# Strassen's seven block products for the down projections of two MLPs and a gated network, in fp32 made of three fp32r products

## The chip, the cores and the metric

One core of one Trainium2 chip runs the whole program. The time is device microseconds of one execution; a kernel's time is the median of its runs.

## The reference

A first block of depth 2 (an even mixer of latent attention and sliding-window attention, an odd mixer of forgetting attention, each followed by an MLP and a gate), then a second block (gated linear attention and a convolution, followed by a gated network). All is float32 over 512 rows of 1024 columns. What the change touches are the three products that take hidden activations back to 1024 columns:

```
def _sq_relu_mlp(x, w_up, w_down):
    return jnp.square(jax.nn.relu(x @ w_up)) @ w_down
...
        x = _layer_norm(DN_ALPHA * x + _sq_relu_mlp(x, w_up[i], w_down[i]), ln2_g[i], ln2_b[i])
...
        h2 = rmsnorm(x, norm2_g[l])
        ffn = (jax.nn.silu(h2 @ w_ffn_gate[l]) * (h2 @ w_ffn_up[l])) @ w_ffn_down[l]
        x = x + ffn
```

`w_up` is 1024 x 4096, `w_down` 4096 x 1024 (twice); the gated network has 2816 hidden columns.

## The kernel before, in words

A float32 matrix is kept as two fp32r ones: hi, a cast made by ScalarE, and lo, the remainder, a subtraction made by VectorE (`split`, L312; the cast is L269, the subtraction L280). A float32 product is three TensorE matmuls, hi x hi, hi x lo and lo x hi (`mm3`, L243; every one is L241), added up in one of eight PSUM banks.

A small planner writes the order of the instructions at build time. Each piece of work is a Python generator (`Core.spawn`) that yields what it waits for; `Core.run` (L362) keeps a clock per engine from assumed costs and takes the next step by when its conditions are met, with a look-ahead of 1400 ns, VectorE and ScalarE work ahead of TensorE work. The engines then run what was written, each in its own order, and wait on semaphores. Memory comes from arenas of columns: `ar_t` and later `ax_r` for fp32r (L495: NR = 118 x 256 and NX = 24 x 256 columns), `af_t` for float32.

`Weights` (L409) brings weights in the order of a plan: `loads` (L425) issues a 512 KB DMA on SyncE into a raw float32 tile while fewer than `rawcap` (2) are held, `preps` (L440) splits a raw tile into a unit (hi and lo, 1024 columns each, 2048 columns in all) while fewer than `cap` units are in use, `get` and `done` hand it out and take it back. Four units are fixed; more come from the arena if there is room. In the MLPs the cap is 8.

An MLP (`mlp`, L1279) goes in four quarters of 1024 hidden columns, called parts here; the gated network (`ffn`, L1996) in three, of 8, 8 and 6 column tiles. So there are 4 + 4 + 3 = 11 parts. In a part, first eight tiles of 128 hidden columns are made for all 512 rows: eight triples of matmuls by `fm` (L580), then `up_ev` (L1292): relu on ScalarE out of PSUM, square on VectorE, split into H (the tile's hi and lo, 512 columns each). Then the products: for each half of the output columns (h) and each block of 128 rows (t), `tm` (L593) makes eight triples of 128x512 matmuls with H as the stationary operand and eight weight tiles moving, 24 matmuls a block, 192 a part. `resid` (L626) adds the block to the residual in `xt` on VectorE (L294). Behind the last part `ln_finish` (L614) normalizes, and a gate layer follows.

Of the kernel before, what the change touches and what calls it, by code (L numbers as in the profile page):

```python
# [17 lines left out]
D = 1024  # L18
# [125 lines left out]
class Core:  # L144
# [91 lines left out]
    def mm(self, out, lhsT, rhs, start, stop):  # L236
# [4 lines left out]
        self.nc.tensor.matmul(out, lhsT, rhs, start=start, stop=stop)  # L241

    def mm3(self, out, sh, sl, mh, ml, start, stop):  # L243
        self.mm(out, sh, mh, start, False)
        self.mm(out, sh, ml, False, False)
        self.mm(out, sl, mh, False, stop)
# [162 lines left out]
class Weights:  # L409


    def __init__(self, core, cap):
        self.c, self.cap = core, cap
        self.plan, self.units, self.inuse = [], {}, 0
        self.raws = {}
        self.rawcap, self.closed = 2, False
        self.fixed = [core.ar.take(2048, 0) for _ in range(4)]
        self.home = list(self.fixed)
        self.rawfix = [core.af.take(1024, 0) for _ in range(2)]
        self.rawhome = list(self.rawfix)  # L420

    def add(self, key, src, d0, d1):
        self.plan.append((key, src, d0, d1))

# [14 lines left out]

    def preps(self):  # L440
        c = self.c
        i = 0
        while True:
            yield ("x", [lambda: len(self.plan) > i or self.closed])
            if i == len(self.plan):
                return
            key, src, d0, d1 = self.plan[i]
            i += 1
            n = d0 * d1
            yield ("x", [lambda: key in self.raws and self.inuse < self.cap])  # L450
            self.inuse += 1
            raw = self.raws[key]
# [12 lines left out]
            if raw in self.rawfix:  # L465
                self.rawhome.append(raw)
            else:
                raw.free()
            del self.raws[key]
# [17 lines left out]
def model_kernel(ctx: ExitStack, tc: tile.TileContext, a: dict, dbg=None):  # L487
# [7 lines left out]
    NR, NF, NS, NX = 118 * 256, 60 * 256, 4 * 256, 24 * 256  # L495
# [782 lines left out]

    def mlp(i, pT):  # L1279
        pT["b"] = yield from c.allocs(R, 1024, 2)  # L1280
        H = (yield from c.allocs(R, 1024, 8))
        hv = [z.v(2) for z in H]

        def hcols(n, t):
            return [(z[:, 0, tb(t)], z[:, 1, tb(t)]) for z in hv[:n]]

        he = {}
        g = yield from bcast(a["ln2_g"][i], D)
        b_ = yield from bcast(a["ln2_b"][i], D)
        st = [small(12) for _ in range(NB)]  # L1290

        def up_ev(b, f, e, dn):  # L1292
# [6 lines left out]
            c.split(hv[f][:, 0], hv[f][:, 1], r.ap)  # L1299
# [5 lines left out]
        ev = None  # L1305
        e0 = [[None] * 4, [None] * 4]
        for q in range(4):
            es = [Event() for _ in range(8)]
            f0 = 0
            if q == 0:  # L1310
                f0 = 4
                yield from first([("up", i, 0, f) for f in range(f0)],
                                 lambda n, b: c.spawn(up_ev(b, n, es[n], dn_done), 0))
            for f in range(f0, 8):
                w = yield from W.get(("up", i, q, f))
                b = yield from fm(w, 0, 128, A["x"], 8, A["ev"])
                W.done(("up", i, q, f))
                c.spawn(up_ev(b, f, es[f], dn_done), 0)
            if q == 3:
                ev = refresh_A()  # L1320
                c.spawn(pT_load(i, pT), 400)
            dn_done = Event()
            for h in range(2):
                keys = [("dn", i, q, h, u) for u in range(4)]
                for t in range(NB):
                    b = yield from tm(hcols(8, t), keys, 512, es, t == 3)
                    last = q == 3
                    post = (lambda t=t: ln_finish(t, st[t], g.ap, b_.ap, ev[t])) if last and h else None
                    e = Event()
                    pre = [x for x in (e0[h][t], e0[0][t] if h else None) if x is not None]  # L1330
                    c.spawn(resid(b, t, h, ALPHA if q == 0 else 1.0, st[t] if last else None,
                                  lambda pre=pre: all(x.on for x in pre), post, e), 0)
                    e0[h][t] = e
            dn_done.set()
        for z in H:
            z.free()
# [8 lines left out]
    def pT_load(i, st):  # L1345
        pb = st["b"]
# [649 lines left out]
    def ffn():  # L1996
        H = (yield from c.allocs(R, 1024, 8))
        hv = [z.v(2) for z in H]

        def hcols(n, t):  # L2000
            return [(z[:, 0, tb(t)], z[:, 1, tb(t)]) for z in hv[:n]]

        nf = yield from bcast(a["norm_f_g_2"], D)
        e0 = [[None] * 4, [None] * 4]
# [11 lines left out]
        def up_ev(b, st, f, e, dn):  # L2016
# [3 lines left out]
            c.give(b)  # L2020
            yield ("x", [r.ap])
            c.split(hv[f][:, 0], hv[f][:, 1], r.ap)
            r.free()
            e.set()

        for q in range(3):
            nk = 8 if q < 2 else 6
            es = [Event() for _ in range(nk)]
            f0 = 0
            if q == 0:  # L2030
                f0 = 2
                sts = [{"e": Event()} for _ in range(f0)]

                def evac(n, b):
                    f = n // 2
                    c.spawn(up_ev(b, sts[f], f, es[f], dn_done) if n % 2 else silu_ev(b, sts[f]), 0)

                yield from first([(nm, f) for f in range(f0) for nm in ("fg", "fu")], evac)
            for f in range(f0, nk):
                st = {"e": Event()}  # L2040
                for nm in ("fg", "fu"):
                    w = yield from W.get((nm, q * 8 + f))
                    b = yield from fm(w, 0, 128, A["x"], 8, A["ev"])
                    W.done((nm, q * 8 + f))
                    c.spawn(silu_ev(b, st) if nm == "fg" else up_ev(b, st, f, es[f], dn_done), 0)
            dn_done = Event()
            for h in range(2):
                keys = [("fd", q, h, u) for u in range(nk // 2)]
                for t in range(NB):
                    b = yield from tm(hcols(nk, t), keys, 512, es, t == 3)  # L2050
                    post = (lambda t=t: rms_out(t, nf.ap)) if q == 2 and not h else None
                    e = done2[t] if q == 2 and h else Event()
                    pre = [y for y in (e0[h][t], e0[0][t] if h else None) if y is not None]
                    c.spawn(resid(b, t, h, 1.0, None, lambda pre=pre: all(y.on for y in pre), post, e), 0)
                    e0[h][t] = e
            dn_done.set()

    def plan_ffn():
        for q in range(3):
            nk = 8 if q < 2 else 6  # L2060
            for f in range(nk):
                W.add(("fg", q * 8 + f), a["w_ffn_gate_2"][q * 8 + f], 8, 128)
                W.add(("fu", q * 8 + f), a["w_ffn_up_2"][q * 8 + f], 8, 128)
            for h in range(2):
# [4 lines left out]
    def plan_mlp(i):  # L2069
        for q in range(4):  # L2070
            for f in range(8):
                W.add(("up", i, q, f), a["w_up"][i, q * 8 + f], 8, 128)
            for h in range(2):
# [150 lines left out]
```

## Time and profile before

| | |
|---|---|
| median of three runs | 1889.79 us (1889.46 to 1891.51) |
| the profiled execution, its own time | 1889.55 us |
| its span | 1887.8 us |
| TensorE matmul busy | 1868.2 us, 99% of the span |
| VectorE, ScalarE busy | 1019.2 us (54%), 714.5 us (38%) |
| mean granted TensorE clock | 0.996 of full speed |

Durations below are those of the profiled execution. PE is TensorE, PEld its weight loads, DVE VectorE, ACT ScalarE. Matmuls are pipelined, so a record of twelve is 0.16 us longer than the distance to the next twelve; the distance is what a matmul costs. An engine's busy share is an average over stages with different limits, so stages are read by themselves.

### The profile page before, as it was taken

The page shows a single profiled execution, that of the slowest core. Times are in us where ns is not written, and L with a number is a line of the kernel's source. Part 1 is how long each engine was busy: PE and PEld are TensorE (multiplying, and loading weights), DVE is VectorE, ACT ScalarE, POOL GpSimd, SP SyncE. Part 2 cuts the span into 40 slices and gives each one's busy share as a digit, 9 for nine tenths or more (in the row PEclk, how much of TensorE's full clock was granted, in tenths as well). Part 3 has the DMA queues.
Part 4 walks back from the last instruction along what each step waited for, and adds up shares of the span by engine and source line. Part 5 has one row for each costly group of instructions (what it writes and reads, how often), then busy time and mean ns, then how long its engine had stood idle before and what let it go on. Part 6 is the DMA issues. An engine that isn't in the chain of part 4 may idle for free.

```text
span 1887.8 us, 23458 instructions
## 1 busy us (share of the span) xinstructions
PE 1868.2 (99%) x9354; PEld 1563.2 (83%) x9354; DVE 1019.2 (54%) x1677; ACT 714.5 (38%) x1242; POOL 62.3 (3%) x123
## 2 busy tenths in 40 slices
PE   9999999999999999989999999999999999999998
PEld 7876788888888888878988888888889898888887
DVE  4666763433447577777734343476675563333333
ACT  4567242323333365553414132333543243132232
POOL 1000100000001000000000000011010000000000
PEclk9999999999999999999999999999999999999999
DMA  5201343232322222222323232332222343133221
GB/s 175 79 32 55 112 136 100 90 111 67 123 90 87 72 79 89 90 90 89 128 85 123 79 111 90 100 112 71 90 90 79 101 134 101 67 123 101 89 90 45
DMA packets 53741, 178.16 MB, mean 94 GB/s; under 512 B 6456, under 2 KB 9072, under 8 KB 53632
## 3 DMA queue, kind: packets, MB, share of 16 engines
q1 hardware_dynamic: 53632, 176.67, 28.7%
q8 instruction: 73, 1.20, 0.3%
q14 instruction: 36, 0.29, 0.1%
HBM read 174.50 MB, written 2.14 MB: 94 GB/s over the span
## 4 chain that ended last, share of the span: by engine, by line
PE 94%; DVE 3%; POOL 1%; ACT 1%; DMA 1%; issue 0%; SPq 0%; POOLq 0%; ACTq 0%; DVEq 0%
PE ps_t L241 91%; PE ps_t L250 3%; DVE ar_t L280 1%; DVE af_t L294 1%; DVE sm_t L631 1%; POOL sm_t L555 0%; POOL sm_t L554 0%; ACT ar_t L269 0%; DMA af_t<-in_ev_w_kv 0%; DMA af_t<-ed 0%; SPq L310 0%; ACT af_t L265 0%; DVE ar_t L289 0%; DVE af_t L280 0%; DVE sm_t L616 0%
## 5 line engine op out<-in xcount | busy, mean ns | idle before, releaser
L241 PE MATMUL ps_t<-ar_t 128*128 128x512 f32 (+5 forms) x6801 | 1430.5, 367 | 9.7 <-DVE ar_t L280 4.1
L241 PEld LDWEIGHTS ps_t<-ar_t 128*128 128x128 f32 x6801 | 1174.0, 189 | 212.0 <-DVE ar_t L280 6.1
L280 DVE TENSOR_TENSOR ar_t<-af_t,ar_t 128x1024 fp32r<-128x1024 f32 (+7 forms) x370 | 402.9, 1097 | 393.8 <-ACT ar_t L269 390.3
L269 ACT CAST ar_t<-af_t 128x1024 fp32r<-128x1024 f32 (+7 forms) x370 | 348.5, 950 | 671.1 <-PE ps_t L241 458.3
L241 PE MATMUL ps_t<-ar_t,ax_r 128*128 128x512 f32 (+1 forms) x1392 | 335.0, 388 | 0.0
L241 PEld LDWEIGHTS ps_t<-ar_t,ax_r 128*128 128x128 f32 x1392 | 259.6, 188 | 53.1
L294 DVE SCALAR_TENSOR_TENSOR af_t<-af_t,ps_t 128x512 f32<-128x512 f32 (+2 forms) x152 | 98.9, 653 | 212.2 <-PE ps_t L241 206.4
L269 ACT CAST ar_t<-ps_t 64x512 fp32r<-64x512 f32 (+4 forms) x169 | 84.9, 521 | 169.7 <-PE ps_t L250 100.9
L280 DVE TENSOR_TENSOR ar_t<-ps_t,ar_t 64x512 fp32r<-64x512 f32 (+4 forms) x169 | 99.6, 607 | 74.8 <-ACT ar_t L269 73.6
L280 DVE TENSOR_TENSOR af_t<-ps_t,af_t 128x512 f32<-128x512 f32 (+1 forms) x82 | 56.1, 686 | 45.8 <-PE ps_t L241 28.3
L280 DVE TENSOR_TENSOR af_t<-af_t 128x512 f32<-128x512 f32 (+2 forms) x105 | 68.0, 648 | 8.1 <-ACT af_t L265 6.6
L269 ACT CAST ax_r<-af_t 128x512 fp32r<-128x512 f32 (+2 forms) x62 | 38.3, 618 | 86.1 <-DVE af_t L280 84.9
L250 PE MATMUL ps_t<-ident,af_t 128*128 128x128 f32 (+1 forms) x496 | 70.2, 273 | 0.4 <-DVE af_t L294 0.3
L294 DVE SCALAR_TENSOR_TENSOR af_t<-af_t,sm_t 128x512 f32<-128x512 f32 x80 | 56.6, 749 | 24.8 <-POOL sm_t L555 17.8
L265 ACT ACTIVATE af_t<-ps_t 128x512 f32<-128x512 f32 (+2 forms) x110 | 58.2, 530 | 26.4 <-PE ps_t L241 26.2
L250 PEld LDWEIGHTS ps_t<-ident,af_t 128*128 128x128 f32 (+1 forms) x496 | 58.0, 139 | 9.7 <-DVE af_t L294 2.5
L265 ACT ACTIVATE af_t<-af_t 128x512 f32<-128x512 f32 (+4 forms) x48 | 31.6, 667 | 89.7 <-DVE af_t L280 50.0
L554 POOL TENSOR_SCALAR sm_t<-sm_t 128x1 f32<-128x1 f32 (+1 forms) x40 | 17.8, 444 | 1403.9 <-DVE sm_t L616 1107.5
L280 DVE TENSOR_TENSOR ax_r<-af_t,ax_r 128x512 fp32r<-128x512 f32 (+2 forms) x62 | 42.6, 687 | 37.2 <-ACT ax_r L269 37.1
L269 ACT COPY af_t<-ps_t 128x512 f32<-128x512 f32 (+4 forms) x75 | 39.9, 562 | 43.8 <-PE ps_t L241 29.7
L265 ACT ACTIVATE af_t<-af_t,sm_t 128x128 f32<-128x128 f32 (+3 forms) x76 | 42.2, 557 | 23.6 <-DVE sm_t L731 19.2
L241 PE MATMUL ps_t<-af_t,ax_f 128*64 128x256 f32 (+6 forms) x136 | 39.4, 418 | 0.6 <-DMA af_t<-ed 0.6
(97 smaller groups left out, 579.0 us busy)
## 6 DMA issues: line engine op xcount, KB each, us to landing
af_t<-in_w_up SPq DMA_DIRECT2D x64, 512.0 KB, 3.4
af_t<-in_w_down SPq DMA_DIRECT2D x64, 512.0 KB, 3.3
af_t<-in_w_ffn_gate SPq DMA_DIRECT2D x22, 512.0 KB, 3.4
af_t<-in_w_ffn_up SPq DMA_DIRECT2D x22, 512.0 KB, 3.5
af_t<-in_w_ffn_down SPq DMA_DIRECT2D x22, 512.0 KB, 3.4
af_t<-in_ple_w_gate SPq DMA_DIRECT2D x16, 512.0 KB, 3.3
af_t<-in_ev_w_out SPq DMA_DIRECT2D x8, 512.0 KB, 4.1
af_t<-in_od_w_q SPq DMA_DIRECT2D x8, 512.0 KB, 3.5
```

The lines of the kernel that those rows point to most:

```text
L241: self.nc.tensor.matmul(out, lhsT, rhs, start=start, stop=stop)
L250: self.nc.tensor.transpose(out, src, ident)
L265: self.nc.scalar.activation(out, src, func, **kw)
L269: self.nc.scalar.copy(out, src)
L280: self.nc.vector.tensor_tensor(out, a, b, op=op)
L294: self.nc.vector.scalar_tensor_tensor(out, a, s, b, op0=op0, op1=op1)
L554: c.pool(165, [src], [v]).tensor_scalar(out=v, in0=src, scalar1=scale, scalar2=eps, op0=ALU.mult, op1=ALU.add)
L631: c.vec(602, [xt[t][:, hs(h)]], [s6]).bn_stats(s6, xt[t][:, hs(h)])
```

## The change

Eight of the eleven parts (all but the last of each MLP and of the gated network) make their products by Strassen's scheme in Winograd's form. The part's 512 x 1024 hidden block is seen as 2 x 2 blocks of 256 rows and 512 columns, its weight as 2 x 2 blocks of 512 x 512. Seven block products of sums of blocks take the place of eight; each is 2 row halves x 4 column tiles x 3 matmuls.

On the hidden side the column tiles come in pairs (`PAIRS`, 0 with 2, 1 with 3, 4 with 6, 5 with 7); relu and square are both on ScalarE, and `Hidden.sums` makes, for each pair, the splits of the three plain blocks (256 and 512 columns), four sums of 256 columns and their split (1024). On the weight side `Weights.add_seven` keeps eight raw tiles, makes eight subtractions in place on VectorE and splits fourteen units. `seven` makes the products in the order 1, 2, 5, 3, 6, 7, 4 (called products 1 to 7), some going on in a bank that an earlier one has filled, and adds to the residual sixteen times. The `rawcap` is 10 in these parts, the norm's gain and bias are loaded ahead of the last part's products instead of at the MLP's start, `af_t` grows from 60 to 75 x 256 columns, and the tiles for the gate's small projection are taken in the last part.

```
+    def add_seven(self, nm, src):
+        for r, c in ((0, 0), (1, 0), (0, 1), (1, 1)):
+            for g in range(2):
+                self.plan.append((nm + (r, c, g), src(r, c, g), 2, 512))
...
+        b11, b12, b21, b22 = (0, 0), (0, 1), (1, 0), (1, 1)
+        for m, z in ((1, b11), (2, b21)):
+            for g in range(2):
+                split(m, z, g)
+        for g in sub(b11, b12, b11):
+            split(5, b11, g)
+        for g in range(2):
+            split(3, b22, g)
+        for g in sub(b11, b22, b11):
+            split(6, b11, g)
+        for g in sub(b12, b22, b12, (b22,)):
+            split(7, b12, g, True)
+        for g in sub(b21, b21, b11, (b11,)):
+            split(4, b21, g, True)
...
     def preps(self):
...
+            if kind == "sub":
+                d, x, y, free = op
...
+                c.tt(ds, xs, ys, ALU.subtract)
...
+        def sums(self, j, ra, rb, e, dn):
+            hi, lo = self.own[0][j], self.own[1][j]
+            sb = yield from c.alloc(F, 1024)
+            yield ("x", [ra.ap, rb.ap, dn])
+            x, y, z = ra.ap, rb.ap, sb.v(4)
+            c.split(hi[:, 0:256], lo[:, 0:256], x[:, 0:256])
+            c.split(hi[:, 256:768], lo[:, 256:768], y)
+            c.tt(z[:, 0], x[:, 256:512], y[:, 256:512], ALU.add)
+            c.tt(z[:, 2], x[:, 0:256], x[:, 256:512], ALU.subtract)
+            c.tt(z[:, 1], z[:, 0], x[:, 0:256], ALU.subtract)
+            c.tt(z[:, 3], y[:, 0:256], z[:, 1], ALU.subtract)
...
+            c.split(self.sum[0][j], self.sum[1][j], sb.ap)
...
+    def hidden():
+        big = yield from c.allocs(R, 1024, 8)
+        return Hidden(big, (yield from c.allocs(R, 768, 8)))
...
+        def add(self, t, h, src):
+            s, pre, e = self.next(t, h)
+            yield ("x", [pre, src])
+            c.stt(xt[t][:, hs(h)], xt[t][:, hs(h)], s, src, ALU.mult, ALU.add)
...
+        for m, bs in ((1, x), (2, p)):
+            for t in range(2):
+                bs[t] = yield from part(m, t, None, range(3), True)
...
+        for m, bs in ((1, x), (2, p)):
+            for t in range(2):
+                yield from part(m, t, bs[t], [3], False)
+                c.spawn(give(None if m == 1 else bs[t], [acc.add(t, 0, c.pb(bs[t]))], xe[t] if m == 1 else None), 0)
+            done(m)
+        for t in range(2):
+            z[t] = yield from part(5, t, None, range(4), True)
+            c.spawn(give(None, [acc.add(t + 2, 1, c.pb(z[t]))], ze[t]), 0)
+        done(5)
+        for t in range(2):
+            yield from part(3, t, z[t], range(4), False, [ze[t]])
+            c.spawn(give(z[t], [acc.add(t, 1, c.pb(z[t]))]), 0)
+        done(3)
...
+        for t in range(2):
+            yield from part(6, t, x[t], range(4), False, [xe[t]])
+            c.spawn(keep(t), 0)
+        done(6)
+        for t in range(2):
+            yield from part(7, t, x[t], range(4), False, [ue[t]])
+            c.spawn(give(x[t], [acc.add(t + 2, 0, c.pb(x[t])), acc.add(t + 2, 1, c.pb(x[t]))]), 0)
+        done(7)
+        for t in range(2):
+            b = yield from part(4, t, None, range(4), True)
+            c.spawn(give(b, [acc.add(t + 2, 0, c.pb(b))]), 0)
...
     def mlp(i, pT):
-        pT["b"] = yield from c.allocs(R, 1024, 2)
-        H = (yield from c.allocs(R, 1024, 8))
...
-        g = yield from bcast(a["ln2_g"][i], D)
-        b_ = yield from bcast(a["ln2_b"][i], D)
+        H = yield from hidden()
...
+        W.rawcap = 10
...
+            if not last:
+                yield from seven(("dn", i, q), H, es, acc)
```

`keep(t)` copies product 6's bank to SBUF on ScalarE and adds it from there, so that product 7 can go on in the bank.

On VectorE, in the products of part 2 (the first MLP's second quarter), the order before is this, where `ar_t<-af_t,ar_t 128x1024` is the lo half of a weight unit and `af_t<-af_t,ps_t` an add onto the residual:

```order
L294 SCALAR_TENSOR_TENSOR af_t<-af_t,ps_t 128x512 x3
L280 TENSOR_TENSOR ar_t<-af_t,ar_t 128x1024 x2
L294 SCALAR_TENSOR_TENSOR af_t<-af_t,ps_t 128x512
L280 TENSOR_TENSOR ar_t<-af_t,ar_t 128x1024 x2
L294 SCALAR_TENSOR_TENSOR af_t<-af_t,ps_t 128x512 x3
```

In the change the same place begins so, where `af_t<-af_t 128x1024` is a subtraction of two raw weight tiles:

```order
L294 SCALAR_TENSOR_TENSOR af_t<-af_t,ps_t 128x512
L280 TENSOR_TENSOR ar_t<-af_t,ar_t 128x1024 x2
L280 TENSOR_TENSOR af_t<-af_t 128x1024
L294 SCALAR_TENSOR_TENSOR af_t<-af_t,ps_t 128x512 x3
L280 TENSOR_TENSOR ar_t<-af_t,ar_t 128x1024
L280 TENSOR_TENSOR af_t<-af_t 128x1024
L294 SCALAR_TENSOR_TENSOR af_t<-af_t,ps_t 128x512 x2
L280 TENSOR_TENSOR ar_t<-af_t,ar_t 128x1024
L280 TENSOR_TENSOR af_t<-af_t 128x1024
L280 TENSOR_TENSOR ar_t<-af_t,ar_t 128x1024
L280 TENSOR_TENSOR af_t<-af_t 128x1024
L294 SCALAR_TENSOR_TENSOR af_t<-af_t,ps_t 128x512 x2
```

The adds of product 5, the pair in the seventh row, now stand behind the second subtraction for product 6. The first three adds belong to products 1 and 2, with one of product 1 in the first row.

On VectorE, while part 2's hidden columns are made, the order before has for each tile a square, the tile's lo half and a weight's lo half:

```order
L280 TENSOR_TENSOR ar_t<-af_t,ar_t 128x1024
L280 TENSOR_TENSOR af_t<-af_t 128x512
L280 TENSOR_TENSOR ax_r<-af_t,ax_r 128x512
L280 TENSOR_TENSOR ar_t<-af_t,ar_t 128x1024
L280 TENSOR_TENSOR af_t<-af_t 128x512
L280 TENSOR_TENSOR ax_r<-af_t,ax_r 128x512
```

In the change it has for each pair of tiles two lo halves of the plain blocks, four sums of 256 columns and, in the fourth row, the lo half of the sums:

```order
L280 TENSOR_TENSOR ar_t<-af_t,ar_t 128x256
L280 TENSOR_TENSOR ar_t<-af_t,ar_t 128x512
L280 TENSOR_TENSOR af_t<-af_t 128x256 x4
L280 TENSOR_TENSOR ax_r<-af_t,ax_r 128x1024
L280 TENSOR_TENSOR ar_t<-af_t,ar_t 128x1024 x2
L280 TENSOR_TENSOR af_t<-af_t 128x1024
```

The squares have left VectorE, and two weight units follow each pair, with the first subtraction for product 5 behind the second pair.

## Rows read from the trace of the kernel before

**Rows 1.** The page's head: span, and busy time of each engine.
```profile
span 1887.8 us, 23458 instructions
PE 1868.2 (99%) x9354; PEld 1563.2 (83%) x9354; DVE 1019.2 (54%) x1677; ACT 714.5 (38%) x1242; POOL 62.3 (3%) x123
```

**Rows 2.** The page's chain that ended last, shares of the span by engine.
```profile
PE 94%; DVE 3%; POOL 1%; ACT 1%; DMA 1%; issue 0%; SPq 0%; POOLq 0%; ACTq 0%; DVEq 0%
```

**Rows 3.** Stretches of part 2: length, busy time by engine, PEclk, DMA share, GB/s.
```profile
320.00:364.00 44.00, 44.00 (x196) 36.42 (x195) 21.77 (x25) 17.26 (x23) 0.00 (x0) 1.00 0.40 131
364.00:407.00 43.00, 43.00 (x191) 35.63 (x190) 13.61 (x16) 8.49 (x9) 0.00 (x0) 1.00 0.20 62
```

**Rows 4.** Timeline of TensorE in part 2's products: start, length, what, count.
```profile
364.67 2.88 PE L241 MATMUL ps_t<-ar_t,ax_r 128*128 128x512 f32 x12
367.39 2.88 PE L241 MATMUL ps_t<-ar_t 128*128 128x512 f32 x12
370.11 2.88 PE L241 MATMUL ps_t<-ar_t,ax_r 128*128 128x512 f32 x12
...
405.47 4.70 PE L241 MATMUL ps_t<-ar_t 128*128 128x512 f32 x20
```

**Rows 5.** Timeline of ScalarE and VectorE there, idle time before in brackets.
```profile
364.64 1.05 ACT L269 CAST ar_t<-af_t 128x1024 fp32r<-128x1024 f32 x1 [1.87 <-PE ps_t L241]
365.73 1.23 DVE L280 TENSOR_TENSOR ar_t<-af_t,ar_t 128x1024 fp32r<-128x1024 f32 x1 [2.23 <-ACT ar_t L269]
366.87 0.69 DVE L280 TENSOR_TENSOR af_t<-af_t 128x512 f32<-128x512 f32 x1
...
370.31 0.69 DVE L294 SCALAR_TENSOR_TENSOR af_t<-af_t,ps_t 128x512 f32<-128x512 f32 x1 [1.37 <-PE ps_t L241]
```

**Rows 6.** Groups of instructions by shape: count, busy us, mean ns, idle before.
```profile
L280 DVE TENSOR_TENSOR ar_t<-af_t,ar_t 128x1024 fp32r<-128x1024 f32 x289 | 351.5, 1223 | 356.5 <-ACT ar_t L269 353.5
L269 ACT CAST ar_t<-af_t 128x1024 fp32r<-128x1024 f32 x289 | 302.4, 1052 | 600.7 <-PE ps_t L241 456.5 <-DMA af_t<-in_w_up 72.9 <-DMA af_t<-in_w_ffn_gate 21.9
L294 DVE SCALAR_TENSOR_TENSOR af_t<-af_t,ps_t 128x512 f32<-128x512 f32 x136 | 92.8, 684 | 206.4 <-PE ps_t L241 206.4
L265 ACT ACTIVATE af_t<-ps_t 128x512 f32<-128x512 f32 x86 | 50.9, 592 | 16.9 <-PE ps_t L241 16.7
L265 ACT ACTIVATE af_t<-af_t 128x512 f32<-128x512 f32 x34 | 21.2, 630 | 64.5 <-DVE af_t L280 42.9 <-DVE af_t L294 21.6
L269 ACT COPY af_t<-ps_t 128x512 f32<-128x512 f32 x36 | 20.2, 586 | 21.1 <-PE ps_t L250 10.9 <-PE ps_t L241 10.0
L280 DVE TENSOR_TENSOR ax_r<-ps_t,ax_r 128x256 fp32r<-128x256 f32 x28 | 11.7, 418 | 7.5 <-ACT ax_r L269 7.5
```

**Rows 7.** DMA issues of the norms' bias: count, KB each, us to landing.
```profile
af_t<-in_ln_b SPq DMA_DIRECT2D x4, 512.0 KB, 4.8
```

**Rows 8.** Timeline of VectorE behind the first MLP, instructions back to back.
```profile
577.77 2.48 DVE L280 TENSOR_TENSOR ar_t<-ps_t,ar_t 128x512 fp32r<-128x512 f32 x4
...
585.04 2.35 DVE L280 TENSOR_TENSOR ar_t<-af_t,ar_t 128x1024 fp32r<-128x1024 f32 x2
587.31 0.68 DVE L294 SCALAR_TENSOR_TENSOR af_t<-af_t,ps_t 128x512 f32<-128x512 f32 x1
```

**Rows 9.** Timeline of TensorE in the second mixer and the first, its longest waits.
```profile
28.94 1.10 PE L241 MATMUL ps_t<-af_t,ax_f 128*128 128x512 f32 x2 [0.56 <-DMA af_t<-ed]
...
822.02 0.57 PE L241 MATMUL ps_t<-ar_t 128*128 128x128 f32 x2 [3.31 <-DVE ar_t L289]
...
843.55 0.44 PE L241 MATMUL ps_t<-ar_t 128*128 128x128 f32 x2 [2.96 <-DVE ar_t L280]
```

**Rows 10.** Stretches behind these waits, columns as in rows 3.
```profile
822.00:828.00 6.00, 5.98 (x28) 4.59 (x28) 5.84 (x15) 2.33 (x6) 0.00 (x0) 0.72 0.13 27
844.00:852.00 8.00, 7.63 (x31) 5.98 (x31) 7.94 (x18) 4.40 (x10) 0.00 (x0) 0.57 0.20 68
20.00:30.00 10.00, 9.37 (x39) 6.71 (x39) 1.67 (x8) 2.76 (x7) 0.74 (x2) 1.00 0.59 159
```

More of the change, by code (lines that the diff above doesn't have):

```diff
@@ L234, in size, with mm @@
         return n
-    def mm(self, out, lhsT, rhs, start, stop):
+    def mm(self, out, lhsT, rhs, start, stop, more=False):
         n = self.size(rhs)
@@ L438, in loads, with drop_raw @@
             self.raws[key] = raw
+    def drop_raw(self, key):
+        raw = self.raws.pop(key)
+        if raw in self.rawfix:
+            self.rawhome.append(raw)
+        else:
+            raw.free()
     def preps(self):
@@ new lines, in down @@
+    def down(keys, H, nk, es, acc, sts=None, post=None, ends=None):
+        for h in range(2):
+            for t in range(NB):
+                b = yield from tm(H.cols(nk, t), keys[h], 512, es, t == 3)
+                s, pre, e = acc.next(t, h)
+                both = acc.done[t][0]
+                if ends is not None and h:
+                    e = acc.done[t][h] = ends[t]
+                c.spawn(resid(b, t, h, s, sts[t] if sts else None,
+                              lambda pre=pre, both=both, h=h: pre() and (not h or both.on),
+                              post(t, h) if post else None, e), 0)
@@ L2020, in up_ev, with pair, evac @@
             c.give(b)
+            if e is None:
+                st["e2"].set()
+                return
             yield ("x", [r.ap])
[L2022 removed]
+            c.split(H.plain[f][:, 0], H.plain[f][:, 1], r.ap)
             r.free()
             e.set()
[L2026 to L2028 removed]
+        def pair(j, sts, e, dn):
+            p, q = (sts[f] for f in PAIRS[j])
+            yield ("x", [p["e2"], q["e2"]])
+            yield from H.sums(j, p["r"], q["r"], e, dn)
+        ready = Event()
+        ready.set()
+        for q in range(3):
+            last = q == 2
+            nk = 6 if last else 8
+            order = range(6) if last else FORDER
+            es = [Event() for _ in range(nk if last else 4)]
+            sts = {f: {"e": Event(), "e2": Event()} for f in range(8)}
+            def evac(n, b, es=es, sts=sts, dn=dn_done):
+                f = order[n // 2]
+                if n % 2 == 0:
+                    c.spawn(silu_ev(b, sts[f]), 0)
+                    return
+                c.spawn(up_ev(b, sts[f], f, es[f] if last else None, dn if last else ready), 0)
+                if not last and n % 4 == 3:
+                    c.spawn(pair(n // 4, sts, es[n // 4], dn), 0)
             f0 = 0
@@ L2031, in ffn @@
                 f0 = 2
[L2032 to L2045, printed above, removed]
-            dn_done = Event()
[L2047 to L2055, printed above, removed]
+                yield from first([(nm, f) for f in order[:f0] for nm in ("fg", "fu")], evac)
+            for n in range(2 * f0, 2 * nk):
+                key = (("fg", "fu")[n % 2], q * 8 + order[n // 2])
+                w = yield from W.get(key)
+                b = yield from fm(w, 0, 128, A["x"], 8, A["ev"])
+                W.done(key)
+                evac(n, b)
+            dn_done = Event()
+            if not last:
+                yield from seven(("fd", q), H, es, acc)
+            else:
+                W.rawcap = 2
+                yield from down([[("fd", q, h, u) for u in range(nk // 2)] for h in range(2)], H, nk, es, acc, None,
+                                lambda t, h: None if h else (lambda: rms_out(t, nf.ap)), done2)
             dn_done.set()
```

201 lines of the change are left out of this document (147 added, 54 removed).

## The prediction, before the run

> **What bounds the kernel now.** I read the page's first lines, then the chain of waits, then the stretches around one part of the first MLP, and last the timeline of that part. The page has TensorE busy 99% of a span of 1887.8 us [rows 1], and the chain that ended last is 94% TensorE [rows 2], so time leaves the kernel when matmuls leave it, as long as nothing new makes TensorE wait. The reader should see in the two stretches that one part has two halves of unlike slack: while the hidden columns are made VectorE works 21.77 of 44 us, while the products behind them run it works 13.61 of 43 us [rows 3]. The change puts nearly all its new work on VectorE, and most of it into the second stretch. The timeline there shows twelve 128x512 matmuls start every 2.72 us without a gap from 364.67 to 405.47 [rows 4]: 0.2267 us each, whichever operand is in which arena. A part's products are 192 of them, 43.5 us.
>
> **What goes away.** Each of the eight parts makes 7 products of 2 x 4 x 3 = 24 matmuls, 168 for 192. The order confirms it for the whole program: 128x512 matmuls from 5078 + 1368 to 5094 + 1160, 192 fewer. At 0.2267 us that is 43.5 us, all on TensorE, which is the path. A part's products would take 38.1 us, and the kernel 1889.55 - 43.5 = 1846.0 us if nothing else moved (1889.55 is the profiled execution's own time, 0.24 below the median of the runs).
> The Trainium skill (TensorE: Matmul & The Clock Gate, Back-to-back issue gap) gives about 131 ns for a sustained 512-column stream and 216 ns for an isolated one; by it the 192 would be worth 25 or 41 us. The rows of this very stream show 226.7 ns, so the measurement decides.
>
> **What comes on top.** Per changed part, by full record lengths [rows 6]: six more weight splits (14 units for 8), 6 x 1.052 us ScalarE and 6 x 1.224 VectorE; eight 128x1024 subtractions, 9.8 VectorE; sixteen adds onto the residual for eight, 8 x 0.684; and each of the four column pairs is split as 256 + 512 + 1024 with four 256-column sums between, where two columns took a 512 square and a 512 split each. The pairs cost 4 x (0.42 + 0.69 + 4 x 0.42 + 1.22) = 16.0 for 8 x (0.69 + 0.69) = 11.0. VectorE so rises by about 27.6 us a part, ScalarE by some 16 (splits, wider casts, two 0.586 copies out of PSUM, the squares). In the feed-forward network the 512 product of gate and up stays on VectorE, 5.5 us more in a longer part. Over a part of 44 + 38 us both engines have room. DMA traffic is the same bytes; the prefetch limit of 10 raw tiles only starts loads earlier. The late loads of the norm's gain and bias still start before the last part's products, whose first block that needs them ends over 20 us later, against 4.8 us to landing [rows 7]. I cost these at nothing; without that cover they are 4.8 us, twice.
>
> Inside the products there is little room. VectorE's order there is 14 lo halves, 6 subtractions and 16 adds. What counts for a queue is the distance of starts. Back to back, two 1024 instructions and the next start lie 2.27 us apart, 1.14 each, and four 512 ones take 2.48, of which the last record is 0.69, so 0.60 each [rows 8]; a 256 one I take as 0.42 - 0.09 = 0.33. In all that gives 20 x 1.14 + 16 x 0.60 = 32.4 of 38.1 us, and a subtraction, ScalarE's hi cast (1.05) and the lo half of one unit are a chain in which VectorE has one or two instructions at most to fill the cast.
> The Trainium skill (VectorE: DVE Perf Modes, The DRAIN you can't avoid) says that the next instruction starts only when the pipe has emptied; by that the full records count, 20 x 1.22 + 16 x 0.69 = 35.4 us. The rows speak against it: 365.73 + 1.23 ends after 366.87, where the next begins [rows 5].
>
> **The walk through one part's products.** T is from the first product matmul; the products run 1, 2, 5, 3, 6, 7, 4, each over two row halves of 2.72 us; m.g is group g of product m's weight. A result reaches VectorE 0.2 us after TensorE goes on (the twelve from 367.39 end in the record at 370.27, the next began at 370.11, the add at 370.31), and a cast ends 0.04 before its lo half [rows 5]. The arena leaves six weight units: 36352 columns less 8192 for the four fixed ones, 8192 for the normalized rows and 14336 for the new column factors leave 5632, two units of 2048. So 3.1 can only be written when product 1 has ended.
> Products 1 and 2 start with three of four column pairs, 8.16 us of cover for the last pair, which needs relu, square, three splits and four sums: ScalarE's cast of 5.1 to 1.2, relu 1.75, square 2.35, the casts of 256 and 512 columns 3.25 (0.9 for three quarters of a 1.052 us cast); VectorE's sums 5.4; cast 6.5; lo half 7.7. That is 0.46 us before it is wanted. I cost it at nothing.
> Then VectorE, in the order shown for part 2, which seven of the eight parts share: first add ready at 9.04, done 9.65; lo of 3.0 10.8; 3.1 (cast from 9.75) 12.0; subtraction for 6.0 13.1; three adds 14.9; lo of 6.0 16.05; subtraction for 6.1 17.2; add of product 5, first half, 17.85. Product 3 accumulates into the bank that this add reads, and TensorE is ready for it at 16.32: it waits until 17.9, **1.6 us**. The rest holds with TensorE 1.6 late: 6.1 done 19.6 (wanted 24.7), 7.0 23.0 (28.8), 7.1 26.45 (30.1), copy of product 6 26.85, 4.0 29.9 (34.2), 4.1 33.25 (35.6). The next part's first units follow at 35.6 and 36.7, before 39.7.
> In part 1 the add of product 5 stands before the subtraction for 6.1 and is done at 15.5, in time; there 4.1 comes 0.45 late.
> The sum of waits is 7 x 1.6 + 0.5 = 11.7 us. Bounds: nothing, if the queue runs a little ahead of my walk; with full record lengths the same walk ends the add at 18.6, a wait of 2.3, in all 17. The forecast is 1846.0 + 11.7 = 1857.7, **1858 us**, 1.7% below, with 1852 to 1866 as this case's own range. A measurement can tell 0.2%, 3.8 us, from no change.
>
> **The rivals.**
> *No wait*: the adds find VectorE free and all 43.5 us come off: 1846. For it: products 5 and 3 leave a half product of cover. Against: seven parts have the subtraction ahead of the add.
> *Two waits a part*: the last pair's 0.46 us of slack is gone as well (ScalarE's cast ahead of the relu waits for the unit just released), 1.3 us more, with 2.3 instead of 1.6 at the add: 3.6 x 8 = 29, 1875.
> *The clock*: before, waits of 3.31 and 2.96 us [rows 9] are followed by stretches at a granted 0.72 and 0.57, that is at 1.2 GHz for a part of them, while a wait of 0.56 us [rows 9] left 1.00 [rows 10]. At the lower level 6 us lose 0.28 x 6 = 1.7, and 8 us lose 3.4. If each part's wait reaches 3 us, that is 8 x (3 + 1.7 to 3.4) = 38 to 51: 1884 to 1897. My 1.6 us lies between the two kinds of row, nearer to the short ones.
> The Trainium skill (TensorE: Matmul & The Clock Gate, HAM oscillation) describes such idle gaps bringing the clock down again and again; the rows after 822 and 844 agree, and no row shows it for a gap of 1.6 us.
> *VectorE as the bound, slower than before*: the place is the last unit, 4.1. Behind its lo half TensorE still has 18 matmuls, 4.1 us; before, the products took 43.5. So the part gains only if 4.1 is ready by T = 39.4; I have 33.25. It decides if the queue runs 6.2 us later than walked: with nothing in the six chains overlapped, 6 x (1.14 + 1.09 + 1.18) + 2 x 1.18 + 16 x 0.72 = 34.3 behind 8.84 ends at 43.2, the part at 47.3, 8 x 3.8 = 30 us slower: 1920. Against it: the order puts adds into the chains.
> *It doesn't do what it says*: the 192 matmuls leave, but the planner lays out the other layers anew and loses as much there: 1886 to 1893. Against: outside the changed parts TensorE's order holds the same instructions, with a few blocks moved.
>
> **How the numbers follow.** Forecast 0.48; no wait 0.16; two waits 0.16; clock 0.10; VectorE as the bound 0.06; the layout 0.04. The range 1845 to 1882 takes in the first three and leaves the last three out, 0.20. Faster by over 0.2% (below 1885.8): the first three, 0.80, 0.04 of the clock's (where not every part reaches it) and 0.01 of the layout's, so 0.85; same: 0.03 of the clock's and 0.02 of the layout's, 0.05; slower: the rest, 0.10.
>
> **What would show it.** Right: 192 fewer 128x512 matmuls; the MLP's twelve still every 2.72 us; a wait of TensorE of 1 to 2 us behind a VectorE add, once a part, at the start of product 3; VectorE over 85% busy in the products. Wrong: no such wait (then 1846), waits at the first products on the last pair's lo half, a granted clock under 1.00 inside the MLPs, or TensorE held at 4.1 or at the next part's first unit.

## The result, and the profile after

The changed kernel takes 1871.42 us (median of four runs, 1870.90 to 1872.28) against 1889.62 for the kernel before on the same chip: a ratio of 0.9902, 95% interval 0.9885 to 0.9919. It is faster by 18.2 us where 31.8 were forecast; 1871.4 lies in the range, but above the 1852 to 1866 that the prediction calls this case's own. The profiled execution took 1871.11 us.

The page's head, which answers to [rows 1]:

```profile
span 1869.4 us, 23488 instructions
PE 1831.6 (98%) x9162; PEld 1528.1 (82%) x9162; DVE 1222.1 (65%) x1965; ACT 816.2 (44%) x1386; POOL 62.5 (3%) x123
```

192 matmuls have gone. But TensorE's busy time fell by 36.6 us and not by 43.5, and its idle time (span less busy) rose from 19.6 to 37.8. VectorE rose by 203 us, 25 a part (the prediction had 27.6 by full record lengths).

The products of part 2 of the first MLP, columns as in [rows 3]:

```profile
359.60:399.30 39.70, 38.20 (x169) 31.34 (x168) 33.49 (x40) 18.29 (x21) 0.00 (x0) 1.00 0.36 133
```

The products take 39.7 us for 43.5, with TensorE idle for 1.5 of them, and VectorE works 33.49 us, 84%, a little under the 85% that the prediction gave as a sign. The granted clock is 1.00.

TensorE's waits over the whole run (total, times, longest; the rows with most):

```profile
PE ps_t L241 <- DVE af_t L294: 10.8, 8, 1.5
PE ps_t L250 <- DMA af_t<-in_p: 5.2, 1, 5.2
PE ps_t L241 <- DVE ar_t L280: 4.7, 6, 3.0
PE ps_t L241 <- DVE ar_t L289: 3.3, 1, 3.3
PE ps_t L250 <- DVE af_t L294: 2.0, 3, 1.6
```

The first row is the forecast one: eight waits behind an add, seven of 1.5 us. The fourth, and most of the third (2.96 us in one), are the second mixer's, as before [rows 9]. The second row, and the 1.64 us in the fifth, are new, and no step of the prediction has them. They lie together behind the second MLP. TensorE's timeline there:

```profile
1234.31 1.04 PE L250 MATMUL ps_t<-ident,af_t 128*128 128x128 f32 x8
1240.53 0.69 PE L250 MATMUL ps_t<-ident,af_t 128*128 128x128 f32 x2 [5.18 <-DMA af_t<-in_p]
1242.85 2.39 PE L250 MATMUL ps_t<-ident,af_t 128*128 128x128 f32 x10 [1.64 <-DVE af_t L294]
...
1252.37 0.73 PE L241 MATMUL ps_t<-ar_t 128*128 128x512 f32 x2 [0.46 <-ACT ar_t L269]
```

SyncE's queue before it (start, time in issue, what):

```profile
1186.22 0.42 SPq L310 DMA_DIRECT2D af_t<-in_ln_b  x1
1234.11 0.33 SPq L310 DMA_DIRECT2D af_t<-in_norm_g  x1
1234.53 0.38 SPq L310 DMA_DIRECT2D af_t<-in_ple_b_gate  x1
1235.01 2.00 SPq L310 DMA_DIRECT2D af_t<-in_p  x1
1237.06 0.90 SPq L310 DMA_DIRECT2D af_t<-in_ple_w_gate  x2
1238.06 7.55 SPq L310 DMA_DIRECT2D af_t<-in_p  x2
```

The queue issues nothing from 1186.6 to 1234.1: the load of the next block's norm gain stands at its head for 47.4 us, until VectorE has read the buffer it goes to. The four loads of the gate's input p are written behind it. So TensorE comes to the transposes of p before p does, and the chain of the layer norm, which the small product with p should have covered, lies bare. Before, the p loads went out in the last part's products, and TensorE had no gap in this place.

### The profile page after: what moved, and what is told of

The parts are those of the page before. It is cut to its first block, busy times and chain, and to the rows that moved or that the text cites. A ratio compares the mean times of both kernels' runs of the same rounds, so it can differ in the third digit from the quotient of the medians.

```text
span 1869.4 us, 23488 instructions
## 1 busy us (share of the span) xinstructions
PE 1831.6 (98%) x9162; PEld 1528.1 (82%) x9162; DVE 1222.1 (65%) x1965; ACT 816.2 (44%) x1386; POOL 62.5 (3%) x123
## 4 chain that ended last, share of the span: by engine, by line
PE 46%; DVE 4%; issue 1%; ACT 0%; POOL 0%; DMA 0%; POOLq 0%; DVEq 0%; ACTq 0%
PE ps_t L241 45%; DVE ar_t L280 1%; DVE af_t L294 1%; DVE af_t L280 1%; PE ps_t L250 0%; ACT ar_t L269 0%; POOL sm_t L601 0%; DMA af_t<-in_w_in_cb 0%; ACT af_t L265 0%; DMA af_t<-in_p 0%; POOL sm_t L600 0%; DVE sm_t L677 0%; DVE ax_r L280 0%; DVE sm_t L662 0%; POOLq L2444 0%
## 5 line engine op out<-in xcount | busy, mean ns | idle before, releaser
L241 PE MATMUL ps_t<-ar_t 128*128 128x512 f32 (+4 forms) x6817 | 1448.0, 367 | 9.9 <-DVE ar_t L280 4.7
L280 DVE TENSOR_TENSOR ar_t<-af_t,ar_t 128x1024 fp32r<-128x1024 f32 (+6 forms) x450 | 471.7, 1062 | 329.4 <-ACT ar_t L269 322.5
L269 ACT CAST ar_t<-af_t 128x1024 fp32r<-128x1024 f32 (+6 forms) x450 | 405.4, 921 | 552.7 <-PE ps_t L241 370.4
L241 PE MATMUL ps_t<-ar_t,ax_r 128*128 128x512 f32 (+1 forms) x1184 | 300.4, 389 | 10.9 <-DVE af_t L294 10.8
L241 PEld LDWEIGHTS ps_t<-ar_t,ax_r 128*128 128x128 f32 x1184 | 220.4, 188 | 61.0 <-issue 14.0
L269 ACT CAST ar_t<-ps_t 128x512 fp32r<-128x512 f32 (+4 forms) x177 | 87.9, 515 | 190.9 <-PE ps_t L250 121.5
L280 DVE TENSOR_TENSOR af_t<-af_t 128x256 f32<-128x256 f32 (+2 forms) x249 | 161.4, 669 | 4.5 <-ACT af_t L265 2.1
L280 DVE TENSOR_TENSOR ar_t<-ps_t,ar_t 128x512 fp32r<-128x512 f32 (+4 forms) x173 | 101.3, 602 | 80.2 <-ACT ar_t L269 79.0
L269 ACT CAST ax_r<-af_t 128x1024 fp32r<-128x1024 f32 (+3 forms) x62 | 51.9, 837 | 76.9 <-DVE af_t L280 74.5
L250 PEld LDWEIGHTS ps_t<-ident,af_t 128*128 128x128 f32 (+1 forms) x496 | 59.7, 143 | 17.3 <-DMA af_t<-in_p 5.9
L600 POOL TENSOR_SCALAR sm_t<-sm_t 128x1 f32<-128x1 f32 (+1 forms) x40 | 18.2, 454 | 1394.7 <-DVE sm_t L662 1089.1
L280 DVE TENSOR_TENSOR ax_r<-af_t,ax_r 128x512 fp32r<-128x512 f32 (+3 forms) x46 | 40.1, 871 | 24.9 <-ACT ax_r L269 24.8
```

The source lines that it names most:

```text
L250: self.nc.tensor.transpose(out, src, ident)
L269: self.nc.scalar.copy(out, src)
L280: self.nc.vector.tensor_tensor(out, a, b, op=op)
L600: c.pool(165, [src], [v]).tensor_scalar(out=v, in0=src, scalar1=scale, scalar2=eps, op0=ALU.mult, op1=ALU.add)
```

## The experiments

The changed kernel's `pT_load` takes two 1024-column tiles of the fp32r arena before it writes its loads. Before, they were taken at the MLP's start. **Theory A**: two losses by two causes. The add ahead of product 3 costs some 12 us, as predicted; the room in the arena costs the rest, at the second gate. **Rivals**: the gate waits for the normalization anyway; it is only the load in front in the queue; the loss belongs to the seven products; or VectorE has no more room, and a wait taken away comes back.

The runs below come from three chips, on which the kernel before took 1889.95, 1888.87 and 1888.35 us; the ratios (and their 95% intervals in brackets) are to the kernel before on the same chip, so they compare better across runs than the times do.

### p loaded early

```
+    # class Hidden
+        def free_own(self):
+            for z in self.bufs[8:]:
+                z.free()
+            self.bufs = self.bufs[:8]
...
                 ev = refresh_A()
+                H.free_own()
                 c.spawn(pT_load(i, pT), 400)
```

> The changed kernel with one edit: before the last part of an MLP the eight 768-column tiles of the column factors, which that part does not use, go back to the arena, so that the gate's two 1024-column tiles find room and its p loads are issued in the last part. Theory A (the arena is full, so the second gate's p loads are issued behind the norm gain's load, and TensorE waits 5.2 + 1.6 + 0.5 us there and runs at a lower clock behind it): the waits on p go, and the time falls by 9 to 11 us, from 1871.4 to 1860 to 1862. Theory B (the normalization's own chain on VectorE and GpSimd bounds the start of the second gate, p or no p): the wait on p turns into a wait on the normalized rows and the time stays within 3 us of 1871.

Measured 1859.94 us, ratio 0.9843 (0.9828 to 0.9857): 11.5 us less than the changed kernel (11.1 by the ratios). Two stretches at the second gate, columns as in [rows 3], in the changed kernel:

```profile
1228.00:1238.00 10.00, 7.35 (x37) 5.96 (x35) 9.46 (x13) 6.35 (x8) 1.68 (x2) 1.00 0.29 85
1238.10:1248.40 10.30, 6.16 (x21) 4.55 (x21) 9.76 (x16) 2.86 (x5) 1.69 (x2) 0.50 0.44 161
```

The same stretches in this kernel, whose MLP begins 1.8 us later:

```profile
1228.00:1238.00 10.00, 10.00 (x54) 8.41 (x53) 9.25 (x15) 4.90 (x6) 1.85 (x3) 1.00 0.03 5
1238.10:1248.40 10.30, 10.30 (x50) 8.33 (x50) 9.75 (x13) 3.86 (x6) 1.69 (x2) 1.00 0.44 149
```

And its queue on SyncE:

```profile
1191.16 7.67 SPq L310 DMA_DIRECT2D af_t<-in_p  x3
...
1236.95 0.33 SPq L310 DMA_DIRECT2D af_t<-in_norm_g  x1
```

The norm gain still waits, to 1236.95, and now nothing that TensorE needs soon stands behind it. TensorE is busy throughout. The loss is made of the three waits, 5.18 + 1.64 + 0.46 = 7.3 us, and of 6.16 us of work at the lower level of the clock (0.50, 1.2 GHz), which cost half of it, 3.1. Together 10.4 of the 11.5 measured; the rest is less than this kernel's runs differ by (1859.57 to 1861.63). With p there, TensorE waits for nothing at the gate, so the normalization does not bound it.

### Only the norm gain earlier

```
                 b_ = yield from bcast(a["ln2_b"][i], D)
+                if i == 1:
+                    pT["n1"] = yield from bcast(a["norm1_g_2"], D)
...
-        n1 = yield from bcast(a["norm1_g_2"], D)
+        n1 = pT["n1"]
```

> The changed kernel with one edit: the next block's norm gain is loaded beside the second MLP's own gain and bias; the p loads stay where they were, behind it. If the queue is what counts (the norm gain's load stands in SyncE's queue for 47.4 us, until a buffer is read, and holds up p), p lands before TensorE wants it and the time falls to 1860 to 1864. If room in the arena is what counts (the p loads cannot go earlier whatever stands ahead of them, because their tiles or the gate's bias must wait as well), p is still late and the time stays at 1868 to 1872.

Measured 1871.68 us (0.9889 to 0.9922): nothing gained. The norm gain went out at 1186.16, and the gate's bias took its place at the head of SyncE's queue (its timeline, columns as above):

```profile
1186.16 0.42 SPq L310 DMA_DIRECT2D af_t<-in_norm_g  x1
1233.58 0.33 SPq L310 DMA_DIRECT2D af_t<-in_ple_b_gate  x1
1234.00 0.38 SPq L310 DMA_DIRECT2D af_t<-in_p  x1
```

TensorE waits on p three times there, 3.89, 2.42 and 1.09 us. So it does not matter which of the two loads stands in front: the p loads are written late, behind whichever of them waits.

### Room for p and no more

```
-            for z in self.bufs[8:]:
-                z.free()
+            own = sorted(self.bufs[8:], key=lambda z: z.lo)
+            for z in own[:3]:
+                z.free()
...
```

> As the run with p loaded early, but only three of the eight 768-column tiles are given back: 2304 columns, room for the two tiles of p (2048) and for no further weight unit. Theory A (the 11.5 us between the changed kernel and that run came from the room for p alone): the same time, 1859 to 1861, no wait on p. Rival (the further weight units that all eight tiles make room for carried part of it): 1863 to 1870, with waits on weights in the last part or at the gate.

Measured 1860.09 us, ratio 0.9845 (0.9829 to 0.9862), as with all eight tiles, and no wait on p. Room for two tiles is the cause.

### Plain products, all else as changed

```
-                yield from seven(("dn", i, q), H, es, acc)
+                yield from down([[("dn", i, q, h, u) for u in range(4)] for h in range(2)], H, 8, es, acc)
```

The same is done in the gated network, with the square on VectorE as in the kernel before.

> The changed kernel with plain products in all eleven parts (192 matmuls again in each of the eight, no sums, no subtractions of weights); all else stays: the big column factors in the arena, ten raw tiles, the late gain and bias, the late tiles for p. Theory A (the loss at the second gate belongs to memory and load order, not to Strassen's products): SyncE's queue has the p loads behind the norm gain as in the changed kernel, TensorE waits about 5 us on p, and the time is 1889.6 + 9 to 12 = 1899 to 1902. Rival (that loss comes with the seven products): 1888 to 1892.

Measured 1909.63 us (1.0090 to 1.0120). The direction is theory A's, the size is not: 20.0 us over the kernel before. Here p is late at both gates. SyncE's queue at the first one:

```profile
536.84 0.33 SPq L310 DMA_DIRECT2D af_t<-in_ln_b  x1
583.15 0.33 SPq L310 DMA_DIRECT2D af_t<-in_ple_b_gate  x1
583.59 0.37 SPq L310 DMA_DIRECT2D af_t<-in_p  x1
```

TensorE waits 6.9 us on p there and 5.1 at the second gate. In the changed kernel `pT_load` found room in time at the first gate (its p loads go out from 523.16) and not at the second. Why it is so at one gate and not at the other was not tested.

> The kernel with plain products in all eleven parts once more, but with the unused 768-column tiles given back before the last part of each MLP, as in the run with p loaded early. Theory A (the 20 us that the kernel without Strassen's products lost come from p's late loads at both gates): the p loads go out in the last parts, the waits on p go, and the time is that of the kernel before, 1888 to 1892. Rival (ten raw tiles, the late gain and bias or the other layout cost something by themselves): 1893 to 1905.

With `free_own` as above this kernel takes 1889.38 us, ratio 1.0003 (0.9993 to 1.0012). The ten raw tiles and the late gain and bias cost nothing that these runs can tell.

### A bank of its own for product 3

```
-            c.spawn(give(None, [acc.add(t + 2, 1, c.pb(z[t]))], ze[t]), 0)
+            c.spawn(give(z[t], [acc.add(t + 2, 1, c.pb(z[t])), acc.add(t, 1, c.pb(z[t]))]), 0)
...
-            yield from part(3, t, z[t], range(4), False, [ze[t]])
-            c.spawn(give(z[t], [acc.add(t, 1, c.pb(z[t]))]), 0)
+            b = yield from part(3, t, None, range(4), True)
+            c.spawn(give(b, [acc.add(t, 1, c.pb(b))]), 0)
```

> The changed kernel with one edit: product 3 gets a bank of its own instead of going on in product 5's; product 5's bank is added twice instead of once, 16 more adds in the program. Theory A (TensorE waits for the add only because product 3 writes the same bank): the seven waits of 1.5 us (1.65 by the distance of starts) and the 0.36 go, 11 to 12 us, so 1859.5 to 1861. Rival (VectorE's queue is the limit in the products, and the wait comes back at product 6, 7 or 4, the more so with 1.2 us more adds a part): 1867 to 1875, with TensorE held by a lo half later in the part.

Measured 1885.32 us (0.9970 to 0.9989), slower than either expectation. Two things lie on top of each other: the planner's order moved, and p is late at both gates in this kernel. So the edit was made again on the kernel with p early:

> The kernel with p loaded early (1859.9) plus the bank of its own for product 3. Theory A (with the bank free the wait at product 3 goes, but VectorE's queue then brings the lo half of the last unit, 4.1, too late: in the run with its own bank TensorE waited 1.59 us there, at T about 34, behind four adds): one wait moves in for the other, seven of 1.6 us and a little more in part 1, so 1859 to 1863. Rival (the loss of that run came from the two gates alone and the bank's gain is whole): 1848 to 1851.

Measured 1865.52 us, ratio 0.9876 (0.9861 to 0.9890): 5.6 us worse than without the bank (6.2 by the ratios), 2.5 over the expectation. The waits at product 3 are gone, and one comes in their place. TensorE's timeline in part 2 of this last kernel:

```profile
400.64 58.55 PE L241 MATMUL ps_t<-ar_t 128*128 128x512 f32 x257 [1.57 <-DVE ar_t L280]
```

VectorE's, in the same place:

```profile
396.98 2.47 DVE L294 SCALAR_TENSOR_TENSOR af_t<-af_t,ps_t 128x512 f32<-128x512 f32 x4
399.37 3.49 DVE L280 TENSOR_TENSOR ar_t<-af_t,ar_t 128x1024 fp32r<-128x1024 f32 x3
```

The lo half at 399.37 is that of unit 4.1, behind four adds, and TensorE is there 1.57 us earlier. This is the place that the prediction's rival on VectorE named. So far one wait has moved in for the other. What comes on top lies in two places: part 1, with waits of 0.32, 0.76, 0.28 and 1.88 us, and the gated network's first part, with one of 1.94. Behind both the clock falls (stretches, columns as in [rows 3], and the TensorE row of the second):

```profile
310.00:320.00 10.00, 7.83 (x27) 5.75 (x26) 10.00 (x12) 4.84 (x5) 0.00 (x0) 0.83 0.57 217
1625.00:1635.00 10.00, 9.05 (x33) 7.26 (x34) 9.08 (x9) 4.34 (x5) 0.00 (x0) 0.83 0.69 246
1625.95 14.41 PE L241 MATMUL ps_t<-ar_t 128*128 128x512 f32 x55 [1.94 <-DVE ar_t L280]
```

### The subtractions ahead of the splits

```
-        for g in sub(b11, b22, b11):
+        for g in list(sub(b11, b22, b11)):
             split(6, b11, g)
```

The same for products 5, 7 and 4, on the kernel with p early. In the kernels above a unit's subtraction, cast and lo half follow one another at 3.48 us a unit, since the next subtraction is written behind the lo half; here both subtractions stand in front.

> The kernel with p loaded early plus another order of the weight work: for products 5, 6, 7 and 4 both subtractions are written ahead of both splits, so that one unit's cast runs beside the other's subtraction. Product 3 stays in product 5's bank. Theory A (two separate limits: the add before product 3, and the chain of subtraction, cast and lo half, 3.48 us a unit, before unit 4.1): as many VectorE instructions stand ahead of product 5's add as before, so the wait at product 3 stays at 1.4 to 1.6 us and the time at 1858 to 1861, though the last lo half is done about 3 us earlier. Rival (the chain alone makes the wait): the wait falls under 0.5 us, 1848 to 1852.

Measured 1871.68 us, ratio 0.9908 (0.9893 to 0.9922): slower by 11.7 than with p early alone (12.3 by the ratios), which neither expected. The wait of 1.49 us at product 3 is there, as theory A had it, and a second one behind it, for the other row half. TensorE in part 2 (in part 1 the two are 1.49 and 2.05, where there had been 0.36):

```profile
380.75 2.08 PE L241 MATMUL ps_t<-ar_t,ax_r 128*128 128x512 f32 x8 [1.49 <-DVE af_t L294]
...
384.67 2.14 PE L241 MATMUL ps_t<-ar_t,ax_r 128*128 128x512 f32 x8 [0.91 <-DVE af_t L294]
```

VectorE there:

```profile
379.93 0.68 DVE L294 SCALAR_TENSOR_TENSOR af_t<-af_t,ps_t 128x512 f32<-128x512 f32 x1
380.53 1.21 DVE L280 TENSOR_TENSOR ar_t<-af_t,ar_t 128x1024 fp32r<-128x1024 f32 x1
381.66 2.35 DVE L280 TENSOR_TENSOR af_t<-af_t 128x1024 f32<-128x1024 f32 x2
383.93 0.68 DVE L294 SCALAR_TENSOR_TENSOR af_t<-af_t,ps_t 128x512 f32<-128x512 f32 x1
```

Product 5's second add now stands behind the two subtractions for product 7 (381.66). I had counted what lies ahead of the first add only.

### Both, and another order of the products

> Both edits on the kernel with p loaded early: product 3 in a bank of its own and the subtractions of a product ahead of its splits. Theory A (the add and the chain before 4.1 are two limits one behind the other, and nothing else is within 2 us of TensorE): no wait over 0.4 us in any part, the 12.4 us (seven times 1.65 and part 1's) come off, 1847 to 1849. Rival (VectorE as a whole has no more room in the products, 32 to 34 of 38 us and 1.2 us more by the extra adds): waits of 1 us or more stay behind a lo half, 1855 to 1865.

Measured 1847.10 us, ratio 0.9778 (0.9761 to 0.9794). No wait over 0.24 us is left in any part's products. Part 2's products (columns as in [rows 3]):

```profile
359.80:397.90 38.10, 38.10 (x170) 31.54 (x169) 34.05 (x42) 18.28 (x21) 0.00 (x0) 1.00 0.39 150
```

That is the 38.1 us of 168 matmuls, with VectorE at 89%. VectorE has the room; what it lacked was the order.

The last run keeps product 3 in product 5's bank and makes product 6 before it:

```
-        for g in range(2):
-            split(3, b22, g)
         for g in list(sub(b11, b22, b11)):
             split(6, b11, g)
+        for g in range(2):
+            split(3, b22, g)
```

The matmuls of product 6 move ahead of product 3's in `seven` likewise.

> The kernel with p loaded early and the subtractions ahead of the splits; in place of the bank of its own, products go 1, 2, 5, 6, 3, 7, 4, so that 5.44 us more lie between product 5 and product 3. Its VectorE order has both subtractions for product 6 ahead of the last pair's sums (2.3 us), where the prediction had 0.46 us of slack, and the trace of the changed kernel 0.6. Theory A (that slack is real and small): the waits at product 3 go, and TensorE waits 0.4 to 1.2 us for the last pair's lo half in each of the eight parts, so 1850 to 1857. Rival (VectorE's idle time ahead of the sums takes the subtractions in): no wait, 1846 to 1849.

Measured 1846.83 us, ratio 0.9777 (0.9763 to 0.9792): no wait, so the rival's number was right. Its reason was not: VectorE's idle time does not take the subtractions in. In part 2 the lo half of the last pair's sums is in VectorE's record at 367.37 and the next starts at 368.52, where TensorE is 9.2 us into the products. By the prediction product 1 wants it at 8.16. But products 1, 2 and 4 read the splits of the plain blocks alone:

```
        def factor(self, m, j, t):
            k = SEVEN[m] * 256
            z, k = (self.own, k) if k < 768 else (self.sum, k - 768)
```

`SEVEN` numbers the products 1, 2, 4, 5, 6, 7, 3, so the first three come from `own`. The sums are first read by product 5, 48 matmuls or 10.88 us on, which comes to its last pair nine matmuls later, at 12.9. So TensorE went through product 1's last pair at 8.16 without a stop while that lo half was still in work. VectorE there:

```profile
367.37 1.22 DVE L280 TENSOR_TENSOR ar_t<-af_t,ax_r 128x1024 fp32r<-128x1024 f32 x1 [1.11 <-ACT ax_r L269]
368.52 0.68 DVE L294 SCALAR_TENSOR_TENSOR af_t<-af_t,ps_t 128x512 f32<-128x512 f32 x1
```

This run and the one above beat both the kernel before and the changed one.

## Why the prediction was right or wrong

**The 43.5 us: right.** Where no wait is left the kernel takes 1847.1 or 1846.8; the prediction had 1846.0. Against the kernel before on the same chips these are 41.8 and 41.5 us less, and the intervals (38.9 to 45.1, 39.3 to 44.8) take in 43.5.

**The wait at product 3: right, in place and size.** In the changed kernel TensorE stops once a part at the start of product 3, for 1.50 us against 1.6, and for 0.36 in part 1, where another 0.33 was lost at unit 4.1 as walked (0.45). VectorE's order and times in part 2 follow the walk:

```profile
368.61 0.69 DVE L294 SCALAR_TENSOR_TENSOR af_t<-af_t,ps_t 128x512 f32<-128x512 f32 x1 [1.50 <-PE ps_t L241]
369.21 2.39 DVE L280 TENSOR_TENSOR ar_t<-af_t,ar_t 128x1024 fp32r<-128x1024 f32 x2
371.52 1.22 DVE L280 TENSOR_TENSOR af_t<-af_t 128x1024 f32<-128x1024 f32 x1
372.66 1.87 DVE L294 SCALAR_TENSOR_TENSOR af_t<-af_t,ps_t 128x512 f32<-128x512 f32 x3
374.45 1.22 DVE L280 TENSOR_TENSOR ar_t<-af_t,ar_t 128x1024 fp32r<-128x1024 f32 x1
375.59 1.22 DVE L280 TENSOR_TENSOR af_t<-af_t 128x1024 f32<-128x1024 f32 x1
376.72 1.27 DVE L294 SCALAR_TENSOR_TENSOR af_t<-af_t,ps_t 128x512 f32<-128x512 f32 x2
...
391.94 1.22 DVE L280 TENSOR_TENSOR ar_t<-af_t,ar_t 128x1024 fp32r<-128x1024 f32 x1 [0.51 <-ACT ar_t L269]
```

With the first add at T = 9.04, T = 0 is at 359.57. The add that is waited for ends at 376.72 + 0.60, T = 17.75 (walked 17.85); the lo half of 4.1 starts at 391.94 and ends at T = 33.5 (33.25). The walk by the distance of starts held over 34 us within 0.3. The Trainium skill (VectorE: DVE Perf Modes, The DRAIN you can't avoid), read by the sentence that the prediction takes from it, would have put full records there; the same section adds that a next instruction that is not held back starts earlier, and the trace agrees with that: 371.52 + 1.22 ends after 372.66, where the next begins. All waits of this kind together cost 1859.94 - 1847.10 = 12.8 us (12.3 by the ratios, the two runs being from two chips); the sum had 11.7. A wait's record is a little shorter than what it takes: from product 3 of part 2 to that of part 3 are 83.4 us, for 360 matmuls of 0.2267, 81.6.

**What failed: the loads that the change moves past.** The steps that failed are "I cost these at nothing", which counts the late loads of gain and bias (they did cost nothing) and leaves out those of p, and "Against: outside the changed parts TensorE's order holds the same instructions, with a few blocks moved". The diff has the line that moves p's tiles into the last part, and SyncE's order shows the p loads behind the norm gain. The prediction names neither. Its own sum of the arena shows the want: 5632 columns less two units of 2048 leave 1536, and p's two tiles take 2048. It argued from what TensorE does, while what had moved was when a load is written. This term is 11.5 us, measured by giving the room back. The rival on the layout (0.04) is what happened, at one gate of two, beside the forecast and not in its place; its own price, all 43.5 us, was far off.

That 1871.4 lies in the range at all is luck. The forecast was too low, and the range reaches up to 1882 to take in two waits a part at 1875, which did not happen; the loss that did happen, 13.7 above the forecast, is of like size to that rival's 17.3.

Put together: 1857.7 forecast + 11.5 for p + 1.1 for the waits + 1.1 for the base = 1871.4. This sum must come out, since its terms are differences of the same measured times. What checks it is the trace: 10.4 us at the gate, and for the waits 83.4 - 81.6 = 1.8 us in seven parts, with 0.36 and 0.33 in part 1, an estimate of 13.

**Two waits a part: wrong in its reason.** The 0.46 us of slack at the last pair counted the sums as wanted by product 1. In the changed kernel too they are done at about T = 7.5, product 5 starts at 10.88, and the last pair's are wanted at 12.9, so no wait could arise there. Its lo half, and the first matmuls that read sums:

```profile
365.88 1.23 DVE L280 TENSOR_TENSOR ar_t<-af_t,ax_r 128x1024 fp32r<-128x1024 f32 x1 [1.12 <-ACT ax_r L269]
370.45 1.98 PE L241 MATMUL ps_t<-ar_t,ax_r 128*128 128x512 f32 x8
```

**The clock: right that waits of this kind leave it alone, wrong on where it falls.** It stays at 1.00 in all the MLP parts of the changed kernel. It falls to 0.50 at the gate, while TensorE stands in the wait of 5.18 us, stays there over the stretch of ten microseconds shown above, and costs 3.1 us. With product 3 in a bank of its own it fell inside the parts too, behind waits of 1.88 and 1.94 us.

**VectorE as the bound: not in this kernel, but nearer than it looked.** Unit 4.1 had 2 us to spare because TensorE had been held up by 1.6 us before. Once that wait goes, the same unit is late (own bank), unless the chain of subtraction, cast and lo half is shortened too.

## What to carry to other kernels

When a change takes memory, ask of every allocation that moves which loads are written behind it, and of each such load which waiting load it now follows in its queue: here a layer that the change did not touch paid 11.5 us for two tiles that came late. A wait that has been found may cover the next one; try the cure of both together before judging either, since each cure alone cost time here (5.6 and 11.7 us) and the two together gained 12.8. An operand is wanted when the first instruction that reads it runs, not when a planner's event says that the whole group is there.

## What the runs showed of the hardware

Waits of 1.5 us once in 83 us left the granted clock at 1.00 over the part. In the kernel with p early and a bank of its own for product 3, waits of 1.57 to 1.65 us left it at 1.00 too, but a single one of 1.94 us, with no other in the 100 us on either side, was followed by 0.83 over the stretch from 1625 to 1635, that is by the lower level, 1.2 GHz, for a part of it. Four near one another (0.32, 0.76, 0.28 and 1.88 us, the last ending at 315.55) gave 0.83 over the stretch from 310 to 320. With the subtractions ahead, 1.49 and 2.05 us five microseconds apart in part 1 left 1.00:

```profile
300.00:310.00 10.00, 9.91 (x44) 8.21 (x45) 10.00 (x12) 5.59 (x7) 0.00 (x0) 1.00 0.97 356
```

So a wait can bring the clock down that is shorter than the 2.96 and 3.31 us of [rows 9], and a longer one than 1.94 can leave it. Neither the length of a wait nor the nearness of several decides it by itself in these runs; what does, they don't tell.

A 512 KB load of w_down took 3.3 us from issue to landing in the kernel before (median of its 64) and takes 5.9 in the changed one, where up to ten raw tiles can be on their way (with plain products and ten raw tiles 4.7, and 4.8 with p early). No wait of TensorE in any run is put down to one of them.
